# Keys, queries and values kept as hi and lo parts in DRAM between the projections and the attentions

## The chip, the cores and the metric

The kernel runs on one core of a Trainium2 chip. The metric is device time in microseconds (us) of one execution. Before the change three runs took 2356.87, 2360.24 and 2360.92 us; the median is 2360.24 us.

## The reference, cut to what matters

One layer of a streaming encoder in float32, over 1024 prompt frames and 64 sample frames; the sample frames have 512 cached frames behind them.

```python
h = x + 0.5 * post1(swiglu1(pre1(x)))                # 1024 -> 2816 -> 1024
u = pre_mix(h)
c_q, c_kv, k_r, q_sb, k_sb, v_sb = split(u @ w_in)   # 256, 128, 32, 512, 512, 512 columns
q = rmsnorm(c_q) @ w_uq                              # 8 heads of 64 + 32; the 32 are rotated by position
latent, krope = rmsnorm(c_kv), rope(k_r)             # the sample frames have the cache in front of theirs
o_mla = softmax(mask((q_nope.(latent @ w_uk) + q_rope.krope) * MLA_SCALE)) @ (latent @ w_uv)
z = q_sb.k_sb * SB_SCALE                             # 8 stick-breaking heads of 64
o_sb = exp(log_sigmoid(z) + tail) @ v_sb             # tail: sums of log_sigmoid(-z) from the later keys
h = h + post_mix(concat(rmsnorm(o_mla), rmsnorm(o_sb)) @ w_out)
y = final(h + 0.5 * post2(swiglu2(pre2(h))))
```

The new rows of latent, krope, k_sb and v_sb are outputs too.

## The kernel before

**Precision.** A float32 matmul is done as three matmuls in float32r, on a hi part (the value cast) and a lo part (the value less its hi part): hi·hi, hi·lo and lo·hi (`mm3`). `split` makes the two parts of a tile: ScalarE casts the hi part (L139, or L142 with a scale), VectorE subtracts (L140, or L143 with a scale). Whatever enters a matmul passes through a split; weights do so in each use, in pieces of 128x512 (`unit`, `weight`: load `wr`, split into `wh` and `wl`).

**Order of the work.** The tokens form two groups: the first 512 prompt frames and the 64 sample frames (576), then the other 512 prompt frames. The order is: first feed-forward of group 1, group 1's projections beside group 2's feed-forward, attention 0 (group 1: per head pair and kind two prompt heads over 512 keys and two sample heads over 576 keys), output product 0, group 2's projections, attention 1 (group 2: 16 heads over 1024 keys) beside group 1's second feed-forward, output product 1, and the dense rest. A feed-forward is a generator of single matmuls. While it serves as "filler", `wait(t)` takes matmuls from it until the kernel's own estimate of TensorE's clock reaches t; that happens wherever the code, by its written estimates, would have to wait: for a bank that is being evicted (`bank_m`, with the time that `evict(n)` puts down for n columns), and for the next step of an attention (`attend`). So the order on TensorE is set by these estimates. A tile scheduler then merges the streams of each engine.

**Queues.** Every DMA is issued by one queue, SP's, in the order of the program. A load whose buffer is still in use holds up all that stand behind it, filler weights too.

**Projections** (`project`, `cached`, `latent_kv`). A stage evicts its result to a tile `e` (four buffers) and stores it to DRAM, in full precision: `qm` (rotated queries of the latent heads), `qs` (queries of the stick-breaking heads), `kn`, `kr` (latent keys, rotated part), `ks`, `vm`, `vs` (keys and values). The cached rotated keys, keys and values are copied from DRAM to DRAM (`late`, L124 to L126). The cached latents go through `latent_kv`; its evictions are L518 and L529.

**Attention.** `load_head` loads the operands of a head, one head ahead of its use: `load_keys` loads keys into `kl`, twice, in rows 0 to 63 and again in the rows below (for latent heads the rotated part fills rows 64 to 127), and splits them into `kh` and `kl`; `load_values` loads values and splits them; `prompt_ops` and `sample_ops` load the queries and split them with the scale. Stick-breaking queries have hi in rows 0 to 63 and lo in rows 64 to 127 of one tile, so that one matmul of 128 rows serves two of the three products. Key and query tiles have 4 buffers in attention 0 and 2 in attention 1. On VectorE the splits stand in one queue with the softmax and the scan of the stick-breaking weights (`a`, L619 and L622), with the lo part of turned weights (`pl`, L680), and with the filler's splits.

Of the kernel before, what the change touches and what calls it, by code (L numbers as in the profile page):

```python
# [65 lines left out]
class Layer:  # L66
    def __init__(self, tc, ctx, a):
        self.tc, self.nc, self.a = tc, tc.nc, a
        nc = self.nc
        self.const = ctx.enter_context(tc.tile_pool(name="const", bufs=1))  # L70
        nc.scalar.preload_act_table_set("natural_log_exp_and_others")
        self.turn = 0
        self.free = [0.0] * 5
        self.busy = self.there = 0.0
        self.clock = 0.0
        self.filler = iter(())
        self.mixed = False
# [23 lines left out]
        self.qm = [scratch(f"qm_{g}", [HEADS, P, T]) for g, (_, T, _) in enumerate((G1, G2))]  # L101
        self.qs = [scratch(f"qs_{g}", [512, T]) for g, (_, T, _) in enumerate((G1, G2))]

        self.kn = [scratch(f"kn_{g}", [512, T]) for g, T in enumerate((576, 512, 512))]
        self.kr = [scratch(f"kr_{g}", [32, T]) for g, T in enumerate((576, 512, 512))]
        self.ks = [scratch(f"ks_{g}", [512, T]) for g, T in enumerate((576, 512, 512))]
        self.vm = [scratch(f"vm_{g}", [T, 512]) for g, T in enumerate((576, 512, 512))]
        self.vs = [scratch(f"vs_{g}", [T, 512]) for g, T in enumerate((576, 512, 512))]
# [8 lines left out]
    def late(self):  # L117
        nc, a = self.nc, self.a
        self.small = self.load("small", [P, 8])
        self.ident = self.load("ident", [P, P])  # L120
        self.blk = self.load("blk", [P, P])
        self.tri = self.load("tri", [P, P])
        self.osg = self.load("osg", [P, 8])
        nc.sync.dma_start(self.kr[2], a["c_kr"])  # L124
        nc.sync.dma_start(self.ks[2], a["c_k"])
        nc.sync.dma_start(self.vs[2], a["c_v"])  # L126
# [249 lines left out]
    def project(self, gi, g, hi, lo, pool, ev, tmp, at):  # L376
# [44 lines left out]
        nc.sync.dma_start(self.kr[gi], kro)  # L421


        def stick_proj(m):
            wh, wl = self.weight(pool, a["win"][3 + m])
            e = tmp()
# [5 lines left out]
            rows = slice((m % 4) * P, (m % 4) * P + P)  # L432
            if m < 4:
                nc.sync.dma_start(self.qs[gi][rows], e)
            else:
                nc.sync.dma_start(self.ks[gi][rows], e)
                nc.sync.dma_start(a["o_k"][rows, t0:t0 + T], e)

# [3 lines left out]
        for m in range(2):  # L442
# [3 lines left out]
            for h in range(4):  # L446
# [9 lines left out]
                nc.sync.dma_start(self.qm[gi][4 * m + h], e)  # L456
# [18 lines left out]
        for half in range(2):  # L475
            wv = [self.weight(pool, a["wv"][2 * half + i]) for i in range(2)]
            cols = slice(half * 256, half * 256 + 256)
            for i, n in nt:
# [11 lines left out]
                nc.sync.dma_start(self.vs[gi][i:i + n, cols], e[:n])  # L490
# [18 lines left out]
    def latent_kv(self, ev, tmp, wh, wl, lah, lal, T, C, si):  # L509
        nc = self.nc  # L510
        for m in range(4):
            e = tmp()[:, :T]
            ws = slice(m * P, m * P + P)
            for c0 in range(0, T, C):
# [3 lines left out]
                nc.any.tensor_copy(e[:, cs], ps[:, :C])  # L518
                self.evict(C)
            nc.sync.dma_start(self.kn[si][m * P:m * P + P], e)  # L520
        for i in range(0, T, P):
# [6 lines left out]
            e = tmp()[:, :512]  # L528
# [5 lines left out]
    def load_keys(self, pool, kind, h, parts):  # L534
# [4 lines left out]
        c = 0  # L539
        for src in parts:  # L540
            if kind == "mla":
                kn, kr = src
                n = kn.shape[1]
                nc.sync.dma_start(f(lo[0:64, c:c + n]), kn[h * HD:h * HD + HD])
                nc.sync.dma_start(f(lo[64:96, c:c + n]), kr)
                nc.sync.dma_start(f(lo[96:128, c:c + n]), kr)
            else:
                n = src.shape[1]
                nc.sync.dma_start(f(lo[0:64, c:c + n]), src[h * HD:h * HD + HD])
                nc.sync.dma_start(f(lo[64:128, c:c + n]), src[h * HD:h * HD + HD])  # L550
            c += n
        self.split(hi[:, :c], lo[:, :c])
        return hi, lo

    def load_values(self, pool, pair, parts):
# [4 lines left out]
        for src in parts:  # L560
            n = src.shape[0]
            full = n // P
            cols = slice(pair * P, pair * P + P)
            if full:
                for h in range(2):
                    hc = slice(pair * P + h * HD, pair * P + h * HD + HD)
                    nc.sync.dma_start(f(v[:, t:t + full, h, 1]),
                                      src[0:full * P, hc].rearrange("(t p) d -> p t d", p=P))
                    self.split(v[:, t:t + full, h, 0], v[:, t:t + full, h, 1])
            t += full  # L570
            if n % P:
                m = n % P
                nc.sync.dma_start(f(v[0:m, t, :, 1]), src[full * P:, cols].rearrange("k (h d) -> k h d", h=2))
                self.split(v[0:m, t, :, 0], v[0:m, t, :, 1])
                t += 1
# [231 lines left out]
    def load_head(self, pool, gi, pair, kind, what, par):  # L807
# [3 lines left out]
        if what == "sample":  # L811
            vsrc = [self.vm[2], self.vm[0][512:576]] if mla else [self.vs[2], self.vs[0][512:576]]
            v = self.load_values(pool, pair, vsrc)
            return [self.sample_ops(pool, mla, 2 * pair + p, p) for p in range(2)], v
        if par == 0:
            src = self.vm if mla else self.vs
            v = self.load_values(pool, pair, [src[0][0:512]] + ([src[1]] if gi else []))
        return self.prompt_ops(pool, mla, 2 * pair + par, gi), v

    def prompt_ops(self, pool, mla, h, gi):  # L820
        nc = self.nc
        if mla:
            parts = [(self.kn[0][:, 0:512], self.kr[0][:, 0:512])] + ([(self.kn[1], self.kr[1])] if gi else [])
        else:
            parts = [self.ks[0][:, 0:512]] + ([self.ks[1]] if gi else [])
        kh, kl = self.load_keys(pool, "mla" if mla else "sb", h, parts)
        ql = pool.tile([P, 512], F32R, name="ql", bufs=self.ahead)
        qh = pool.tile([P, 512], F32R, name="qh", bufs=self.ahead)
        if mla:
            nc.sync.dma_start(f(ql), self.qm[gi][h][:, 0:512])  # L830
            self.split(qh, ql, MLA_SCALE)
        else:
            rows = slice(h * HD, h * HD + HD)
            nc.sync.dma_start(f(ql[0:64]), self.qs[gi][rows, 0:512])
            nc.sync.dma_start(f(ql[64:128]), self.qs[gi][rows, 0:512])
            nc.scalar.activation(qh, f(ql), AF.Copy, scale=SB_SCALE)
            nc.vector.scalar_tensor_tensor(qh[64:128], f(ql[64:128]), SB_SCALE, f(qh[64:128]),
                                           op0=ALU.mult, op1=ALU.subtract)
# [49 lines left out]
    def sample_ops(self, pool, mla, h, par):  # L888

        nc = self.nc  # L890
        if mla:
            parts = [(self.kn[2], self.kr[2]), (self.kn[0][:, 512:576], self.kr[0][:, 512:576])]
        else:
            parts = [self.ks[2], self.ks[0][:, 512:576]]
        kh, kl = self.load_keys(pool, "mla" if mla else "sb", h, parts)
        ql = pool.tile([P, 512], F32R, name="ql", bufs=self.ahead)
# [4 lines left out]
        if mla:  # L901
            nc.gpsimd.memset(f(ql[:, zc]), 0.0)
            nc.sync.dma_start(f(ql[:, qc]), self.qm[0][h][:, 512:576])
            self.split(qh[:, qc], ql[:, qc], MLA_SCALE)
            return (qh[:, 0:P], kh), (ql[:, 0:P], kh), (qh[:, 0:P], kl)
        rows = slice(h * HD, h * HD + HD)
        nc.sync.dma_start(f(ql[0:64, qc]), self.qs[0][rows, 512:576])
        nc.sync.dma_start(f(ql[64:128, qc]), self.qs[0][rows, 512:576])
        nc.scalar.activation(qh[:, qc], f(ql[:, qc]), AF.Copy, scale=SB_SCALE)
        nc.vector.scalar_tensor_tensor(qh[64:128, qc], f(ql[64:128, qc]), SB_SCALE, f(qh[64:128, qc]),  # L910
                                       op0=ALU.mult, op1=ALU.subtract)
# [102 lines left out]
def body(tc, a, ctx):  # L1014
# [82 lines left out]
    def work(pool, T, n=4):  # L1097
# [11 lines left out]
    with tc.tile_pool(name="x0", bufs=1) as xp:  # L1109
# [26 lines left out]
        L.scaled(tmp, get, "pre1", r, *x1)  # L1136
        L.run(zero)
# [154 lines left out]
```

## Time and profile before

| | us |
|---|---|
| median of three runs | 2360.24 |
| profiled execution | 2364.98 |
| its span in the trace | 2363.2 |
| TensorE busy | 2276.1 (96%) |
| VectorE busy | 1427.0 (60%) |
| ScalarE busy | 1282.0 (54%) |
| GpSimd busy | 94.2 (4%) |

The DMA queue moved 268.79 MB, 114 GB/s over the span. The profiler saw one execution; its span lies within the time measured for it. A busy share is an average over the stretches named above: 0 to 480 us first feed-forward, 480 to 528 latent products of the cache, 528 to 672 projections of group 1, 676 to 1020 attention 0, 1210 to 1340 projections of group 2, 1345 to 1800 attention 1, and feed-forward work between and after these.

### The profile page before, as it was taken

The page shows a single profiled execution, that of the slowest core. Times are in us where ns is not written, and L with a number is a line of the kernel's source. Part 1 is how long each engine was busy: PE and PEld are TensorE (multiplying, and loading weights), DVE is VectorE, ACT ScalarE, POOL GpSimd, SP SyncE. Part 2 cuts the span into 40 slices and gives each one's busy share as a digit, 9 for nine tenths or more (in the row PEclk, how much of TensorE's full clock was granted, in tenths as well). Part 3 has the DMA queues.
Part 4 walks back from the last instruction along what each step waited for, and adds up shares of the span by engine and source line. Part 5 has one row for each costly group of instructions (what it writes and reads, how often), then busy time and mean ns, then how long its engine had stood idle before and what let it go on. Part 6 is the DMA issues. An engine that isn't in the chain of part 4 may idle for free.

```text
span 2363.2 us, 37608 instructions
## 1 busy us (share of the span) xinstructions
PE 2276.1 (96%) x13869; PEld 2045.5 (87%) x13869; DVE 1427.0 (60%) x2468; ACT 1282.0 (54%) x2494; POOL 94.2 (4%) x270
## 2 busy tenths in 40 slices
PE   8999999989999999999989999999999989999997
PEld 7999999979987777788778999989898888888885
DVE  5444444664248787755874377878776578444444
ACT  5443334453357777754542478787876445433333
POOL 1000000010000000000110000000000010000001
PEclk8999999999999999999999999999999999999998
DMA  6332222454454434344445532323212334333321
GB/s 204 100 99 85 77 90 73 151 170 135 150 153 126 131 108 125 94 153 124 133 134 184 173 99 75 104 79 98 85 60 87 119 95 140 127 98 95 98 85 36
DMA packets 186614, 268.79 MB, mean 114 GB/s; under 512 B 59216, under 2 KB 68048, under 8 KB 186400
## 3 DMA queue, kind: packets, MB, share of 16 engines
q1 hardware_dynamic: 186432, 266.41, 36.3%
q8 instruction: 109, 1.79, 0.3%
q14 instruction: 73, 0.60, 0.1%
HBM read 227.61 MB, written 40.88 MB: 114 GB/s over the span
## 4 chain that ended last, share of the span: by engine, by line
PE 71%; DVE 11%; ACT 9%; DMA 5%; issue 3%; POOL 1%; SPq 0%; DVEq 0%; ACTq 0%; POOLq 0%
PE f L154 48%; PE s L154 9%; PE v L154 6%; PE t L154 6%; DVE a L613 2%; PE t L158 2%; ACT wh L139 1%; DVE wl L140 1%; ACT a L607 1%; ACT a L609 1%; ACT a L608 1%; DVE a L610 1%; DVE e L263 1%; DVE pl L680 1%; DMA e<-h 1%
## 5 line engine op out<-in xcount | busy, mean ns | idle before, releaser
L154 PE MATMUL f<-xh,wh 128*128 128x288 f32 (+1 forms) x2112 | 695.5, 330 | 7.1 <-ACT xh L139 4.4
L154 PE MATMUL f<-xl,wh 128*128 128x288 f32 (+1 forms) x2112 | 695.9, 330 | 2.6 <-POOL xl L140 2.2
L154 PE MATMUL f<-xh,wl 128*128 128x288 f32 (+1 forms) x2112 | 695.3, 329 | 0.0
L139 ACT CAST wh<-wr 128x512 fp32r<-128x512 f32 x638 | 385.2, 619 | 523.4 <-PE f L154 352.4
L140 DVE TENSOR_TENSOR wl<-wr,wh 128x512 fp32r<-128x512 f32 x638 | 435.9, 698 | 250.6 <-ACT wh L139 217.8
L154 PEld LDWEIGHTS f<-xh,wh 128*128 128x128 f32 x2112 | 397.9, 188 | 37.9 <-ACT xh L139 5.4
L154 PEld LDWEIGHTS f<-xl,wh 128*128 128x128 f32 x2112 | 397.9, 188 | 34.4 <-POOL xl L140 4.0
L154 PEld LDWEIGHTS f<-xh,wl 128*128 128x128 f32 x2112 | 398.2, 189 | 28.4 <-issue 1.7
L154 PE MATMUL f<-hh,wh 128*128 128x288 f32 (+2 forms) x1072 | 351.6, 329 | 8.2 <-DVE y L319 8.0
L154 PE MATMUL f<-hh,wl 128*128 128x288 f32 (+2 forms) x1072 | 352.1, 329 | 0.0
L154 PE MATMUL f<-hl,wh 128*128 128x288 f32 (+2 forms) x1072 | 351.1, 328 | 0.1
L154 PEld LDWEIGHTS f<-hh,wh 128*128 128x128 f32 x1072 | 202.5, 189 | 24.0 <-DVE y L319 9.8
L154 PEld LDWEIGHTS f<-hl,wh 128*128 128x128 f32 x1072 | 202.7, 189 | 14.6 <-issue 1.0
L154 PEld LDWEIGHTS f<-hh,wl 128*128 128x128 f32 x1072 | 202.8, 189 | 13.8 <-issue 1.0
L319 DVE TENSOR_TENSOR y<-f,y 128x288 f32<-128x288 f32 (+2 forms) x248 | 126.9, 517 | 121.7 <-PE f L154 121.3
L364 DVE TENSOR_TENSOR act<-f,act 128x288 f32<-128x288 f32 (+1 forms) x132 | 70.1, 531 | 126.5 <-ACT act L363 126.4
L680 DVE TENSOR_TENSOR pl<-t,ph 128x384 fp32r<-128x384 f32 (+1 forms) x160 | 98.6, 631 | 28.6 <-ACT ph L679 27.4
L365 DVE TENSOR_TENSOR act<-f,act 128x288 f32<-128x288 f32 (+1 forms) x132 | 70.0, 531 | 65.0 <-PE f L154 61.0
L139 ACT CAST hh<-act 128x288 fp32r<-128x288 f32 (+1 forms) x132 | 65.1, 493 | 81.1 <-DVE act L365 80.8
L154 PE MATMUL v<-pl,v 128*128 128x256 f32 x320 | 89.8, 303 | 14.2 <-DVE pl L680 13.3
L679 ACT CAST ph<-t 128x384 fp32r<-128x384 f32 (+1 forms) x160 | 84.3, 543 | 33.3 <-PE t L158 31.3
L158 PE MATMUL t<-c_ident,a 128*128 128x128 f32 x616 | 91.3, 273 | 4.9 <-ACT a L624 4.8
(309 smaller groups left out, 3477.4 us busy)
## 6 DMA issues: line engine op xcount, KB each, us to landing
wr<-in_wg SPq DMA_DIRECT2D x176, 256.0 KB, 2.9
wr<-in_wu SPq DMA_DIRECT2D x176, 256.0 KB, 3.1
wr<-in_wd SPq DMA_DIRECT2D x176, 256.0 KB, 2.9
wr<-in_win SPq DMA_DIRECT2D x44, 256.0 KB, 3.2
kl<-ks SPq DMA_DIRECT2D x64, 128.0 KB, 2.9
wr<-in_wout SPq DMA_DIRECT2D x32, 256.0 KB, 3.0
h<-y SPq DMA_DIRECT2D x16, 288.0 KB, 2.3
p<-in_xT SPq DMA_DIRECT2D x16, 256.0 KB, 3.4
```

Source lines behind the costliest of these rows:

```text
L139: nc.scalar.copy(hi, x)
L140: eng.tensor_tensor(lo, x, f(hi), op=ALU.subtract)
L154: self.nc.tensor.matmul(out, lhsT=lhsT, rhs=rhs, start=start, stop=stop)
L158: self.nc.tensor.transpose(out, x, ident)
L263: self.nc.vector.scalar_tensor_tensor(x, src(k), self.gain(name, k), r, op0=ALU.mult, op1=ALU.mult)
L319: nc.vector.tensor_tensor(yy, ps[:, :C], yy, op=ALU.add)
L364: nc.vector.tensor_tensor(s, pg[:, :C], s, op=ALU.mult)
L365: nc.vector.tensor_tensor(s, pu[:, :C], s, op=ALU.mult)
L607: nc.scalar.activation(av, z, AF.Abs)
L613: nc.vector.tensor_tensor_scan(a[:, 0:n - 1][:, ::-1], zs[:, 1:n][:, ::-1], a[:, 0:n - 1][:, ::-1], BIG, op0=ALU.add, op1=ALU.subtract)
L679: nc.scalar.copy(ph[:, end:], tr[:, end:])
L680: nc.vector.tensor_tensor(pl[:, end:], tr[:, end:], f(ph[:, end:]), op=ALU.subtract)
```

## The change

Each of `qm`, `qs`, `kn`, `kr`, `ks`, `vm` and `vs` becomes a pair of DRAM tensors, a hi and a lo part. The projections split before they store (`keep`: a split and two stores, or a split straight out of the bank of the product), with the scale in the queries. The cached rotated keys, keys and values are loaded in tiles of 128 rows, split and stored (`past`), during group 1's first feed-forward. The attentions load both parts, and no longer split. The tiles `e` of the projections have eight buffers. The number of matmuls stays the same, 13,688; ScalarE's instructions go from 2428 to 2329, VectorE's from 2470 to 2380, and the DMAs of the queue from 1247 to 1644.

```diff
+    def past(self, tmp):
+        for dst, src in ((self.kr[2], a["c_kr"]), (self.ks[2], a["c_k"]), (self.vs[2], a["c_v"])):
+            for i in range(0, src.shape[0], P):
+                n = min(P, src.shape[0] - i)
+                x = tmp()[:n, :512]
+                self.nc.sync.dma_start(x, src[i:i + n])
+                self.keep([d[i:i + n] for d in dst], x, tmp)
+                yield True
+
+    def keep(self, dst, x, tmp, scale=None):
+        n, T = x.shape
+        hi, lo = (tmp()[:n, :T].bitcast(F32R) for _ in range(2))
+        self.split(hi, lo, scale, x=x)
+        self.nc.sync.dma_start(dst[0], f(hi))
+        self.nc.sync.dma_start(dst[1], f(lo))
...
         def stick_proj(m):
...
-                nc.any.tensor_copy(e[:, cs], ps[:, :C])
-                self.evict(C)
+                if m < 4:
+                    self.split(e[:, cs].bitcast(F32R), l[:, cs].bitcast(F32R), SB_SCALE, x=ps[:, :C])
+                    self.evict(2 * C)
+                else:
+                    nc.any.tensor_copy(e[:, cs], ps[:, :C])
+                    self.evict(C)
...
                     nc.vector.tensor_tensor(e[:, cs], ps[:, :C], tab[:, cs], op=ALU.mult)
                     self.evict(C)
-                nc.sync.dma_start(self.qm[gi][4 * m + h], e)
+                self.keep([d[4 * m + h] for d in self.qm[gi]], e, tmp, MLA_SCALE)
...
     def latent_kv(self, ev, tmp, wh, wl, lah, lal, T, C, si):
...
-                nc.any.tensor_copy(e[:, cs], ps[:, :C])
-                self.evict(C)
-            nc.sync.dma_start(self.kn[si][m * P:m * P + P], e)
+                self.split(e[:, cs], l[:, cs], x=ps[:, :C])
+                self.evict(2 * C)
+            for d, x in zip(self.kn[si], (e, l)):
+                nc.sync.dma_start(d[m * P:m * P + P], f(x))
...
-            nc.any.tensor_copy(e[:n], ps[:n])
-            self.evict(512)
-            nc.sync.dma_start(self.vm[si][i:i + n], e[:n])
+            self.keep([d[i:i + n] for d in self.vm[si]], ps[:n], tmp)
+            self.evict(1024)
...
-        self.split(hi[:, :c], lo[:, :c])
+        for i, t in enumerate((hi, lo)):
+            c = 0
+            for keys, rot, cols in parts:
+                n = cols.stop - cols.start
+                rows = keys[i][h * HD:h * HD + HD, cols]
+                nc.sync.dma_start(f(t[0:64, c:c + n]), rows)
+                if rot is None:
+                    nc.sync.dma_start(f(t[64:128, c:c + n]), rows)
+                else:
+                    nc.sync.dma_start(f(t[64:96, c:c + n]), rot[i][:, cols])
+                    nc.sync.dma_start(f(t[96:128, c:c + n]), rot[i][:, cols])
+                c += n
...
-    def work(pool, T, n=4):
+    def work(pool, T, n=8):
...
         L.scaled(tmp, get, "pre1", r, *x1)
+        L.run(L.past(tmp))
         L.run(zero)
```

The queue at the first pair of sample heads of attention 0, before (`vm_91`, `kn_82`, `kr_85` are the cached part, `vm_89`, `kn_80`, `kr_83` the sample frames', `in_wu` a weight of the filler):

```order
L567 DMA v<-vm_91 128x4x64 x2
L573 DMA v<-vm_89 64x2x64
L544 DMA kl<-kn_82 64x512
L545 DMA kl<-kr_85 32x512
L546 DMA kl<-kr_85 32x512
L544 DMA kl<-kn_80 64x64
L545 DMA kl<-kr_83 32x64
L546 DMA kl<-kr_83 32x64
L903 DMA ql<-qm_76 128x64
...
L296 DMA wr<-in_wu 128x512 x2
```

The same place after the change (names that end in h and l are the two parts):

```order
L594 DMA v<-vm_2h 128x4x64 x2
L594 DMA v<-vm_2l 128x4x64 x2
L597 DMA v<-vm_0h 64x2x64
L597 DMA v<-vm_0l 64x2x64
L571 DMA kh<-kn_2h 64x512
L575 DMA kh<-kr_2h 32x512
L576 DMA kh<-kr_2h 32x512
...
L571 DMA kl<-kn_2l 64x512
...
L920 DMA qh<-qm_0h 128x64
L920 DMA ql<-qm_0l 128x64
...
L316 DMA wr<-in_wu 128x512
```

Between two filler weights stand 34 issues where there were 17.

The queue in group 1's first feed-forward, where the cached tensors come in, before:

```order
L124 DMA kr_85<-in_c_kr 16x1024
L125 DMA ks_88<-in_c_k 16x16384
L126 DMA vs_94<-in_c_v 16x16384
L296 DMA wr<-in_wg 128x512 x2
L296 DMA wr<-in_wu 128x512 x2
```

After the change, somewhat later in the same feed-forward (`p` is a tile of its input stage):

```order
L316 DMA wr<-in_wg 128x512 x2
L136 DMA p<-in_c_kr 32x512
L316 DMA wr<-in_wu 128x512 x2
L145 DMA kr_2h<-p 32x512
L146 DMA kr_2l<-p 32x512
L136 DMA p<-in_c_k 128x512
L316 DMA wr<-in_wg 128x512
L145 DMA ks_2h<-p 128x512
L146 DMA ks_2l<-p 128x512
L136 DMA p<-in_c_k 128x512
```

Loads and stores of 128 rows now alternate with the weights of the filler.

ScalarE at the latent products of the cache, before (`s` and `t` are banks, `wh<-wr` a weight's cast):

```order
L139 CAST hh<-act 128x512
L518 COPY e<-s 128x512 x2
L518 COPY e<-t 128x512
L529 COPY e<-t 128x512
L529 COPY e<-s 128x512
L139 CAST wh<-wr 128x512 x2
```

After the change:

```order
L159 CAST hh<-act 128x512
L159 CAST e<-s 128x512 x2
L159 CAST e<-v 128x512
L159 CAST e<-t 128x512
L159 CAST wh<-wr 128x512
L159 CAST e<-t 128x512
L159 CAST e<-s 128x512
L159 CAST wh<-wr 128x512
```

The copies have become the casts of splits in the same order; the subtractions stand on VectorE.

## Rows read from the trace of the kernel before

**Rows 1.** The page's first part: busy us, share, instructions of each engine.

```profile
PE 2276.1 (96%) x13869; PEld 2045.5 (87%) x13869; DVE 1427.0 (60%) x2468; ACT 1282.0 (54%) x2494; POOL 94.2 (4%) x270
```

**Rows 2.** Busy time of each engine by stretch; columns in the first line.

```profile
core 0: us, PE busy (x) PEld busy (x) DVE busy (x) ACT busy (x) POOL busy (x), PEclk, DMA share, GB/s
120.00:180.00 60.00, 60.00 (x455) 60.00 (x455) 28.50 (x52) 26.66 (x55) 1.93 (x2) 1.00 0.30 93
480.00:528.00 48.00, 40.96 (x174) 32.56 (x173) 33.07 (x46) 29.18 (x52) 7.31 (x4) 0.93 0.46 154
528.00:672.00 144.00, 143.84 (x1016) 137.12 (x1015) 45.86 (x79) 46.68 (x93) 0.00 (x0) 1.00 0.44 147
676.00:1020.00 344.00, 335.88 (x1758) 270.47 (x1757) 266.29 (x556) 257.76 (x599) 17.34 (x120) 1.00 0.41 119
1210.00:1340.00 130.00, 127.26 (x706) 109.84 (x705) 52.46 (x84) 43.82 (x82) 2.96 (x2) 1.00 0.49 159
1345.00:1800.00 455.00, 436.51 (x3148) 416.01 (x3147) 354.21 (x582) 357.02 (x640) 14.22 (x93) 1.00 0.29 87
```

**Rows 3.** Waits of TensorE, 676 to 1020: us in total, times, longest.

```profile
PE s L154 <- DVE a L619: 4.5, 11, 0.7
...
PE s L154 <- DVE ql L143: 0.2, 1, 0.2
```

**Rows 4.** Waits of TensorE, 1345 to 1800.

```profile
PE v L154 <- DVE pl L680: 13.0, 24, 1.5
PE t L158 <- ACT a L624: 4.6, 4, 1.6
```

**Rows 5.** Timeline of TensorE near 766: start, length, in brackets idle before.

```profile
766.06 0.39 PE L154 MATMUL f<-hh,wh 128*128 128x512 f32 x1
766.65 0.36 PE L154 MATMUL s<-kh,qh 128*128 128x256 f32 x1 [0.20 <-DVE a L622]
```

**Rows 6.** VectorE by line and shape, 676 to 1020 (busy, mean ns, idle before).

```profile
L140 DVE TENSOR_TENSOR wl<-wr,wh 128x512 fp32r<-128x512 f32 x76 | 51.2, 680 | 5.3 <-ACT wh L139 4.8
...
L140 DVE TENSOR_TENSOR v<-v 128x256 fp32r<-128x256 f32 x32 | 12.8, 416 | 3.3 <-ACT v L139 1.7 <-DMA kl<-kr 1.4
...
L140 DVE TENSOR_TENSOR kl<-kl,kh 128x512 fp32r<-128x512 f32 x16 | 10.9, 679 | 1.7 <-ACT kh L139 1.7
```

**Rows 7.** VectorE by line and shape, 1345 to 1800.

```profile
L140 DVE TENSOR_TENSOR kl<-kl,kh 128x1024 fp32r<-128x1024 f32 x16 | 19.5, 1221 | 7.6 <-ACT kh L139 4.1 <-DMA wr<-in_wg 1.9 <-DMA kl<-kn 1.3
...
L140 DVE TENSOR_TENSOR v<-v 128x256 fp32r<-128x256 f32 x29 | 11.1, 412 | 0.6 <-ACT v L139 0.5
...
L143 DVE SCALAR_TENSOR_TENSOR ql<-ql,qh 128x512 fp32r<-128x512 f32 x8 | 5.5, 684 | 0.5 <-ACT qh L142 0.5
```

**Rows 8.** VectorE in the projections: 528 to 672, last row 1210 to 1340.

```profile
L454 DVE TENSOR_TENSOR e<-t,tab 128x288 f32<-128x288 f32 x6 | 2.7, 456 | 0.8 <-PE t L154 0.7
L140 DVE TENSOR_TENSOR ll<-e,lh 128x576 fp32r<-128x576 f32 x3 | 2.2, 759 | 0.7 <-ACT lh L139 0.7
...
L454 DVE TENSOR_TENSOR e<-t,tab 128x512 f32<-128x512 f32 x4 | 2.8, 690 | 1.2 <-PE t L154 1.2
```

**Rows 9.** Timeline of TensorE and ScalarE near 490.

```profile
491.81 0.80 PE L154 MATMUL s<-lh,wh 128*128 128x512 f32 x1 [3.81 <-ACT e L518]
...
486.87 0.62 ACT L139 CAST wh<-wr 128x512 fp32r<-128x512 f32 x1 [5.48 <-DMA wr<-in_wg]
```

**Rows 10.** SP's issues, 681 to 692; last row: KB and us to landing.

```profile
681.87 0.99 SPq L567 DMA_DIRECT2D v<-vm  x2
...
691.24 0.84 SPq L296 DMA_DIRECT2D wr<-in_wu  x2
...
kl<-ks SPq DMA_DIRECT2D x64, 128.0 KB, 2.9
```

**Rows 11.** Waits of the DMA queue, 676 to 1020.

```profile
SPq L296 <- DVE wl L140: 80.8, 32, 10.4
```

More of the change, by code (lines that the diff above doesn't have):

```diff
@@ L100, in __init__, with both @@
         self.o_s = [scratch(f"o_{g}", [D, T]) for g, (_, T, _) in enumerate((G1, G2))]
[L101 to L108, printed above, removed]
+        def both(name, shape):
+            return [scratch(name + n, shape) for n in "hl"]
+        self.qm = [both(f"qm_{g}", [HEADS, P, T]) for g, (_, T, _) in enumerate((G1, G2))]
+        self.qs = [both(f"qs_{g}", [512, T]) for g, (_, T, _) in enumerate((G1, G2))]
+        self.kn = [both(f"kn_{g}", [512, T]) for g, T in enumerate((576, 512, 512))]
+        self.kr = [both(f"kr_{g}", [32, T]) for g, T in enumerate((576, 512, 512))]
+        self.ks = [both(f"ks_{g}", [512, T]) for g, T in enumerate((576, 512, 512))]
+        self.vm = [both(f"vm_{g}", [T, 512]) for g, T in enumerate((576, 512, 512))]
+        self.vs = [both(f"vs_{g}", [T, 512]) for g, T in enumerate((576, 512, 512))]
     def load_gains(self):
@@ L420, in project @@
         nc.sync.dma_start(a["o_kr"][:, t0:t0 + T], kro)
-        nc.sync.dma_start(self.kr[gi], kro)
+        self.keep(self.kr[gi], kro, tmp)
         def stick_proj(m):
             wh, wl = self.weight(pool, a["win"][3 + m])
-            e = tmp()
+            rows = slice((m % 4) * P, (m % 4) * P + P)
+            e, l = tmp(), tmp()
             for c0 in range(0, T, C):
@@ L489, in project @@
                 self.evict(256)
-                nc.sync.dma_start(self.vs[gi][i:i + n, cols], e[:n])
+                self.keep([d[i:i + n, cols] for d in self.vs[gi]], e[:n], tmp)
                 nc.sync.dma_start(a["o_v"][t0 + i:t0 + i + n, cols], e[:n])
@@ L511, in latent_kv @@
         for m in range(4):
-            e = tmp()[:, :T]
+            e, l = (tmp()[:, :T].bitcast(F32R) for _ in range(2))
             ws = slice(m * P, m * P + P)
@@ L527, in latent_kv, with load_keys @@
             mm(ps[:n], lhsT=lah[:, i:i + n], rhs=wl[:, 512:], start=False, stop=True)
-            e = tmp()[:, :512]
-            nc.any.tensor_copy(e[:n], ps[:n])
-            self.evict(512)
-            nc.sync.dma_start(self.vm[si][i:i + n], e[:n])
-    def load_keys(self, pool, kind, h, parts):
+            self.keep([d[i:i + n] for d in self.vm[si]], ps[:n], tmp)
+            self.evict(1024)
+    def load_keys(self, pool, h, parts):
         nc = self.nc
@@ L538, in load_keys @@
         hi = pool.tile([P, self.keys], F32R, name="kh", bufs=self.ahead)
[L539 to L551, printed above, removed]
-        self.split(hi[:, :c], lo[:, :c])
+        for i, t in enumerate((hi, lo)):
[10 more added lines that the diff above has]
+                c += n
         return hi, lo
@@ L559, in load_values @@
         t = 0
-        for src in parts:
-            n = src.shape[0]
+        for vals, rows in parts:
+            n = rows.stop - rows.start
             full = n // P
             cols = slice(pair * P, pair * P + P)
[L564 to L575, printed above, removed]
+            for i, src in enumerate(vals):
+                src = src[rows]
+                if full:
+                    for h in range(2):
+                        hc = slice(pair * P + h * HD, pair * P + h * HD + HD)
+                        nc.sync.dma_start(f(v[:, t:t + full, h, i]),
+                                          src[0:full * P, hc].rearrange("(t p) d -> p t d", p=P))
+                if n % P:
+                    nc.sync.dma_start(f(v[0:n % P, t + full, :, i]),
+                                      src[full * P:, cols].rearrange("k (h d) -> k h d", h=2))
+            t += -(-n // P)
         return v
@@ L816, in load_head @@
             src = self.vm if mla else self.vs
-            v = self.load_values(pool, pair, [src[0][0:512]] + ([src[1]] if gi else []))
+            v = self.load_values(pool, pair, [(src[i], slice(0, 512)) for i in range(gi + 1)])
         return self.prompt_ops(pool, mla, 2 * pair + par, gi), v
@@ L821, in prompt_ops @@
         nc = self.nc
[L822 to L827, printed above, removed]
+        keys = self.kn if mla else self.ks
+        kh, kl = self.load_keys(pool, h, [(keys[i], self.kr[i] if mla else None, slice(0, 512)) for i in range(gi + 1)])
+        ql = pool.tile([P, 512], F32R, name="ql", bufs=self.ahead) if mla else None
         qh = pool.tile([P, 512], F32R, name="qh", bufs=self.ahead)
         if mla:
-            nc.sync.dma_start(f(ql), self.qm[gi][h][:, 0:512])
-            self.split(qh, ql, MLA_SCALE)
+            for t, d in zip((qh, ql), self.qm[gi]):
+                nc.sync.dma_start(f(t), d[h][:, 0:512])
         else:
             rows = slice(h * HD, h * HD + HD)
[L834 to L838, printed above, removed]
+            for i, d in enumerate(self.qs[gi]):
+                nc.sync.dma_start(f(qh[64 * i:64 * i + 64]), d[rows, 0:512])
         return kh, kl, qh, ql
@@ L890, in sample_ops @@
         nc = self.nc
[L891 to L896, printed above, removed]
+        keys = self.kn if mla else self.ks
+        kh, kl = self.load_keys(pool, h, [(keys[i], self.kr[i] if mla else None, c)
+                                          for i, c in ((2, slice(0, 512)), (0, slice(512, 576)))])
         qh = pool.tile([P, 512], F32R, name="qh", bufs=self.ahead)
@@ L901, in sample_ops @@
         if mla:
+            ql = pool.tile([P, 512], F32R, name="ql", bufs=self.ahead)
             nc.gpsimd.memset(f(ql[:, zc]), 0.0)
-            nc.sync.dma_start(f(ql[:, qc]), self.qm[0][h][:, 512:576])
-            self.split(qh[:, qc], ql[:, qc], MLA_SCALE)
+            for t, d in zip((qh, ql), self.qm[0]):
+                nc.sync.dma_start(f(t[:, qc]), d[h][:, 512:576])
             return (qh[:, 0:P], kh), (ql[:, 0:P], kh), (qh[:, 0:P], kl)
         rows = slice(h * HD, h * HD + HD)
[L907 to L911, printed above, removed]
+        for i, d in enumerate(self.qs[0]):
+            nc.sync.dma_start(f(qh[64 * i:64 * i + 64, qc]), d[rows, 512:576])
         return (qh[:, 0:P], kh), (qh[:, 0:P], kl)
```

17 lines of the change are left out of this document (9 added, 8 removed).

## The prediction

> **What bounds the kernel now.** I read first the busy times of the whole span: TensorE is busy 2276.1 of 2363.2 us, VectorE 60%, ScalarE 54% [rows 1]. The matmuls stay the same in number and shape, so the change can only add or remove time in which TensorE waits, some 87 us in all. Second, the engines by stretch [rows 2], to see where these waits lie: none in the dense feed-forward (60.00 of 60.00 us), 0.16 us in the first group's projections (528 to 672), 7.0 us in the step before them (480 to 528), 2.7 us in the second group's projections (1210 to 1340), 8.1 us in the first attention (676 to 1020) and 18.5 us in the second (1345 to 1800). In both attentions VectorE is busy 77 to 78% and ScalarE 75 to 78%; in the projections under 41%. Third, whom TensorE waits for in the attentions: almost always a VectorE result, the scan before the next scores (4.5 us in 11 waits) or the lo part of turned weights (13.0 us in 24) [rows 3, 4]. Fourth, single matmuls: one of 512 columns starts 0.22 to 0.23 us after the last, but across a wait that is shown as 0.20 us the next starts 0.59 us later [rows 5]: the page shows 0.16 us too little per wait. With 20 waits in the first attention and 28 in the second, the real losses are about 8.1 + 3.2 = 11.3 us and 18.5 + 4.5 = 23.0 us.
>
> **What the change removes.** In the first attention the eight VectorE rows of splits end with it: 32 of values at 416 ns, 16 of 576-wide and 16 of 512-wide keys, the prompt and sample queries; 52.3 us together, two of them in [rows 6]. VectorE falls from 266.3 to 214.0 us of 344, 77% to 62%. ScalarE loses a cast for each. In the second attention 19.5 us of keys, 11.1 us of values and two rows of 5.5 us of queries, alike, end [rows 7]: 354.2 to 312.6 us of 455, 78% to 69%. These splits are hardly waited for by themselves (TensorE waits once for one, 0.2 us, [rows 3]), so what they cost is that they stand ahead of a scan or a turned tile on VectorE's queue. I bound this from both sides: nothing, if the order of the work makes the waits; all 11.3 and 23.0 us, if load makes them. Between I take the straight line from the nearest quiet stretch, the first projections: 0.11% of idle TensorE at 32% of VectorE [rows 2], against 2.36% at 77% and 4.06% at 78%. At 62% it gives 1.6%, a third less in the first attention, 3.6 of 11.3 us; at 69% 3.3%, a fifth less in the second, 4.5 of 23.0 us. Gain: 8.1 us.
>
> **What it adds in the projections.** The splits return once per tensor, most of them in stretches where both engines have over half their time free. Most cost nothing: the key split of a 128x576 tile (0.76 us, [rows 8]) stands beside 48 matmuls of 288 columns, 6.3 us of TensorE at 0.132 us each (60 us by 455, [rows 2]). Three places are tight.
> - The query stage of the second group: 8 heads, each 6 matmuls of 512 columns, 8 x 6 x 0.225 = 10.8 us of TensorE. VectorE does 8 x 0.69 us of rotation [rows 8], now 8 x 0.69 us of scaled lo parts as well [rows 7], and four weight halves at 0.7 us [rows 6]: 13.8 us, 3.0 us over. Later projections, which ScalarE evicts, can run meanwhile: I take 2 us (0 to 3). In the first group the same sum gives 12.7 us of TensorE against 8 x (2 x 0.46 + 0.76) + 2.8 = 16.2 us, but some 5 us of filler matmuls now stand between (order): 0.5 us (0 to 3.5).
> - The latent products of the cache at 490 us. TensorE stands 3.81 us there, since ScalarE waited 5.48 us for a late weight and the evictions are behind that cast [rows 9]; neither goes. An eviction is now a cast and a subtraction, so a bank comes free 0.7 us later, once: +0.7 us.
> - The cached keys and values, before three copies from DRAM to DRAM, now 9 loads, 9 splits and 18 stores in the first feed-forward. 27 issues of the queue at 0.55 us are 15 us, spread over 16 weight loads, each good for 24 matmuls of 0.132 us, 51 us in all. TensorE has no idle time there [rows 2] and the weights run ahead: 0 (0 to 5).
>
> **What it does to the loads.** DMA issues on the SP queue from the first to the last key load of the first attention go from 276 to 448 (order). A burst of 17 takes from 681.87 to 691.24 us, 0.55 us each [rows 10]: 152 us become 246 us, of 344. The queue is in order, so a filler weight waits behind every key load ahead of it, and the burst for one sample pair doubles from 17 issues, 9.4 us, to 34, 18.7 us. Against it: today the queue stands 80.8 us in this attention only because the weight tiles are still full [rows 11], which is about the 94.6 us added, and the filler needs a unit of 12 matmuls (2.7 us) every 4.5 us (76 in 344 us, [rows 6]), with 8 split and 4 raw units of lead. A key arrives no later than before either, since the split after landing goes (cast and subtraction, 0.62 and 0.68 us, [rows 6, 9]). At the opening, where the lead is smallest, I take 1 us (0 to 9). In the second attention the issues go from 208 to 320 in some 390 us: 45%, no term.
> The Trainium skill (DMA: Bandwidth & Descriptors, "Issuing engines are not separate DMA queues") says that the time to start a DMA on the sequencer is usually small beside the DMA itself. By that rule the opening costs 0 and the sum would be 1 us better; the rows disagree: at 0.55 us per issue, six in a row outlast the landing of one key load, 2.9 us [rows 10].
>
> **Sum.** -3.6 - 4.5 + 2.0 + 0.5 + 0.7 + 1.0 = -3.9 us. The profiled execution took 2364.98 us (span 2363.2), 4.7 us above the median 2360.24 of the three runs. So 2361.1 in a profile, and 2356.3 as a median: 2356 us. A difference under 0.2%, 4.7 us, can't be told from none here.
>
> **Rivals.**
> 1. The stalls fall by more than their share (20%). If half of both losses goes, that is 17 us, and with the costs of 4.2 us, 13 us less: 2347 us. For it: the waits are on VectorE results [rows 3, 4], and splits are a fifth of VectorE's work in the first attention. Against it: in the second they fill 41.6 of 455 us, so few of its 28 waits can have met one.
> 2. The SP queue becomes the bound of the first attention (26%). Place: the change from one kind of head to the next, eight times, where values wait for a buffer and the keys and filler weights are queued behind that wait. It decides once the queue is late by more than its lead of a few units, and a queue that is busy 246 of 344 us catches up slowly. If each change costs 2.5 us of TensorE, that is 20 us, less 8.1 gained, plus 3.2: 15 us more, 2375 us; half of that is 2365 us. For it: the doubled bursts. Against it: the wait of 80.8 us, which is lead that is not used today [rows 11].
> 3. The tensors are split elsewhere but nothing moves (12%): the attentions' waits are set by the order that is written for them, which keeps its estimates of durations, and the projections hide their share. 0 to 2 us either way: 2360 us.
> 4. The forecast (42%): 2349 to 2361 us, half of it below the line of 0.2%.
>
> **Chances and range.** Faster by over 0.2%: 20% of rival 1 and 20 of the forecast's 42, 40%. Within 0.2%: 22 of the forecast and 12 of rival 3, 34%. Slower: rival 2, 26%. The range that leaves out a tenth at either end cuts the far half of rival 1 and the far third of rival 2: 2343 to 2369 us. The forecast's own range is 2349 to 2361.
>
> **What the changed profile would show.** VectorE near 62% and 69% in the attentions, ScalarE about 14 and 9 points lower than today; waits of TensorE on VectorE fewer, about 7.7 and 18.5 us lost in place of 11.3 and 23.0. In the query stages TensorE waits for the rotation's product or its bank, 2 us in the second group. The first feed-forward still without idle time. If rival 2 holds, ScalarE's casts of filler weights wait for their DMA in the first attention, and the queue no longer waits for weight tiles; TensorE then shows waits on a cast or on a key load that no VectorE row explains. The prediction is wrong if TensorE's idle time in the attentions stays as it is while VectorE's load falls as computed, or if the projections lose more than 6 us.

## The result: 60 us slower, nearly all of it in the first attention

The changed kernel took 2418.87 us (median of four runs, 2415.22 to 2421.27), the kernel before 2358.55 us beside it: a ratio of 1.0248, with a 95% interval of 1.0235 to 1.0262 (so for every ratio below). The forecast was 2356 us, its range 2343 to 2369. Of the rivals, the second named the right place and the right sign (the SP queue in the first attention), with 15 us in place of 60.

The page's first part of the changed kernel, to be read against [rows 1]:

```profile
PE 2294.3 (95%) x13869; PEld 2061.3 (85%) x13869; DVE 1390.4 (57%) x2378; ACT 1248.2 (52%) x2395; POOL 93.2 (4%) x270
```

VectorE and ScalarE have less to do, as intended, and the kernel is slower. By stretch, each cut from its first matmul to that of the next (columns as in [rows 2]): the cached latents, projections 0, attention 0, projections 1, attention 1.

```profile
482.00:513.00 31.00, 27.77 (x108) 22.01 (x108) 22.50 (x35) 21.73 (x42) 0.00 (x0) 0.89 0.68 238
513.00:691.00 178.00, 174.51 (x1151) 160.33 (x1151) 85.31 (x141) 75.65 (x149) 7.30 (x10) 1.00 0.57 187
691.00:1052.00 361.00, 316.45 (x1575) 255.04 (x1573) 206.22 (x422) 202.63 (x458) 16.95 (x117) 0.93 0.50 141
1254.00:1417.00 163.00, 158.08 (x911) 138.69 (x910) 80.87 (x128) 72.40 (x142) 6.42 (x4) 0.99 0.60 198
1417.00:1849.00 432.00, 411.33 (x2967) 393.94 (x2966) 308.83 (x507) 315.29 (x555) 14.15 (x92) 1.00 0.40 118
```

The two attentions of the kernel before, cut in the same way:

```profile
684.00:1004.00 320.00, 312.27 (x1640) 251.65 (x1639) 254.31 (x535) 242.22 (x569) 17.15 (x117) 1.00 0.41 118
1351.00:1794.00 443.00, 425.06 (x3063) 404.81 (x3062) 344.09 (x567) 347.59 (x624) 14.22 (x93) 1.00 0.29 86
```

Attention 0 takes 361 us in place of 320, with 65 matmuls fewer (filler that now runs elsewhere, some 15 us at 0.23 us each). TensorE is idle 44.6 us in place of 7.7, and its granted clock is 0.93 in place of 1.00. VectorE's load fell to 57% and TensorE waits for it all the same, for the scan 23.0 us where it was 4.5 in [rows 3] (us, times, longest):

```profile
PE s L174 <- DVE a L643: 23.0, 11, 3.1
PE v L174 <- DVE pl L704: 6.3, 5, 1.5
PE f L174 <- ACT wh L159: 3.8, 4, 1.6
```

Attention 1 is idle 20.7 us as against 17.9, with VectorE at 71%, down from 78%.

**Where an idle stretch comes from.** TensorE in the changed kernel, after the first pair of latent heads (start, length; in brackets the idle time before):

```profile
726.57 0.28 PE L174 MATMUL s<-kl,qh 128*128 128x256 f32 x1
729.51 0.58 PE L174 MATMUL s<-kh,qh 128*128 128x256 f32 x1 [2.66 <-DVE a L643]
729.89 0.41 PE L174 MATMUL s<-kl,qh 128*128 128x256 f32 x1
733.37 0.66 PE L174 MATMUL s<-kh,qh 128*128 128x384 f32 x1 [3.07 <-DVE a L643]
...
737.78 0.63 PE L174 MATMUL f<-xl,wh 128*128 128x512 f32 x1
738.20 0.63 PE L174 MATMUL f<-xh,wl 128*128 128x512 f32 x1
...
740.41 0.39 PE L174 MATMUL f<-xh,wh 128*128 128x512 f32 x1
740.64 0.39 PE L174 MATMUL f<-xl,wh 128*128 128x512 f32 x1
```

Three blocks of scores follow each other with no filler between, so TensorE stands through the whole chain from scores to scan (L643 is the scan, L619 before), 2.7 and 3.1 us. After it, matmuls of 512 columns start 0.42 us apart, at a granted clock of 0.50 (the level of 1.2 GHz), and 0.23 us apart from 739.5 on, at 1.00. In the kernel before, two score blocks at this place:

```profile
721.46 0.28 PE L154 MATMUL s<-kl,qh 128*128 128x256 f32 x1
...
726.81 0.34 PE L154 MATMUL s<-kh,qh 128*128 128x384 f32 x1
```

Seventeen matmuls of the filler stand between them, and TensorE doesn't wait. SP in the changed kernel at the same time:

```profile
724.39 0.60 SPq L856 DMA_DIRECT2D qh<-qs_0l  x1
728.83 0.34 SPq L765 DMA_DIRECT2D o<-osq  x1
729.26 0.88 SPq L316 DMA_DIRECT2D wr<-in_wg  x2
730.23 0.86 SPq L316 DMA_DIRECT2D wr<-in_wu  x2
731.18 0.93 SPq L594 DMA_DIRECT2D v<-vs_2h  x2
```

The filler's weights are issued at 729.26, behind the key and query loads and behind a store that waits for a head's result. The order of the program has changed with it: 826 filler matmuls stood between the first and the last score of attention 0, and 763 do now. The queue's own waits in attention 0 (us, times, longest), against [rows 11]:

```profile
SPq L594 <- PE v L174: 36.5, 9, 5.8
SPq L765 <- DVE osq L763: 33.2, 10, 7.6
SPq L316 <- DVE wl L160: 17.2, 17, 3.7
```

The wait for full weight tiles (L316) was this in the kernel before, in the same piece of work (684 to 1004):

```profile
SPq L296 <- DVE wl L140: 73.2, 30, 10.4
```

This wait, which the prediction took for unused lead, has fallen from 73.2 us (80.8 in the longer stretch of [rows 11]) to 17.2. Waits for a value buffer (L594) and for a finished head (L765) have grown, those for key and query buffers have shrunk: all holds other than at weights were 86 us and are 93. What grew is the time of the issues themselves, from 135 us of 320 to 224 of 361. Issues and holds together make long stretches of the queue without a filler weight: by SP's timeline the three longest, the opening included, were 16.0, 15.6 and 12.3 us before, with 12, 27 and 15 issues in them, and are 41.0, 37.6 and 31.6 us now, with 50, 52 and 54. (At the opening that is 27 and 54 between two filler weights; the 17 and 34 given with the change are the part for the sample heads.)

The lead can be counted from the timelines: filler weights issued, less those that the filler's matmuls have used up (12 of 512 columns for each), right to some two units. Its median over attention 0 was 8.5 units before and never under 3; after the change it is 1.7, and under 2 for half of the time, from the opening on. So the queue isn't late in single places: the lead, some 10 units when full, is used up at about 702 us and doesn't rise above 6 again before the end of attention 0.

### The profile page after: what moved, and what is told of

Same layout as the page of the kernel before. It is cut to its first block, busy times and chain, and to the rows that moved or that the text cites. A ratio compares the mean times of both kernels' runs of the same rounds, so it can differ in the third digit from the quotient of the medians.

```text
span 2419.5 us, 37800 instructions
## 1 busy us (share of the span) xinstructions
PE 2294.3 (95%) x13869; PEld 2061.3 (85%) x13869; DVE 1390.4 (57%) x2378; ACT 1248.2 (52%) x2395; POOL 93.2 (4%) x270
## 2 busy tenths in 40 slices
DMA packets 252665, 321.42 MB, mean 133 GB/s; under 512 B 102432, under 2 KB 113440, under 8 KB 252480
## 4 chain that ended last, share of the span: by engine, by line
PE 72%; ACT 10%; DVE 9%; DMA 4%; issue 3%; POOL 1%; SPq 0%; DVEq 0%; ACTq 0%; POOLq 0%
PE f L174 50%; PE s L174 8%; PE v L174 6%; PE t L174 6%; DVE a L637 2%; PE t L178 2%; ACT a L631 1%; ACT wh L159 1%; ACT a L632 1%; ACT a L633 1%; DVE a L634 1%; ACT z L628 1%; DVE wl L160 1%; DVE e L283 1%; DMA e<-h 1%
## 5 line engine op out<-in xcount | busy, mean ns | idle before, releaser
L174 PE MATMUL s<-kh,qh 128*128 128x256 f32 (+3 forms) x224 | 84.0, 377 | 30.6 <-DVE a L643 23.0
L703 ACT CAST ph<-t 128x384 fp32r<-128x384 f32 (+1 forms) x160 | 84.2, 543 | 37.6 <-PE t L178 37.3
```

What stands on the lines that cost most here:

```text
L174: self.nc.tensor.matmul(out, lhsT=lhsT, rhs=rhs, start=start, stop=stop)
L703: nc.scalar.copy(ph[:, end:], tr[:, end:])
```

## The experiments

Each was timed beside the kernel before on the same chip; differences are against that.

**What is taken away, alone (e5).** Attentions without splits; matmuls, loads and projections as before.

```diff
-        self.split(hi[:, :c], lo[:, :c])
-        return hi, lo
+        return lo, lo
...
-                    self.split(v[:, t:t + full, h, 0], v[:, t:t + full, h, 1])
+                    nc.gpsimd.memset(f(v[:, t:t + full, h, 0]), 0.0)
```

> The kernel before without any split in the attentions: keys and queries enter as loaded on both sides of the three products (queries unscaled), and the hi part of values is zero (set by GpSimd), so the lo parts are left out of the arithmetic; matmuls, loads and projections as before. It measures what the change takes away, without what it adds. Theory A (the order of the work makes the waits, not the load of VectorE): 2355 to 2362 us against 2360. Theory B (load makes them, as the prediction took it): 8 us less, 2350 to 2354. Theory C (each wait is a split's): 17 us less or more, below 2345.

Measured: 2356.94 us against 2359.38, ratio 0.999 (0.9981 to 1.0000). Theory A's number came. All splits of both attentions are worth 2.4 us, 0 to 4.5. VectorE's busy time over the whole run fell from 1427.0 to 1347.2 us, 79.8 of the 93.9 that the prediction had computed, and TensorE still stood idle:

```profile
681.00:992.00 311.00, 304.64 (x1618) 249.44 (x1616) 208.69 (x428) 202.35 (x462) 25.43 (x146) 1.00 0.40 120
1341.00:1785.00 444.00, 423.47 (x3068) 408.11 (x3067) 311.09 (x507) 320.01 (x567) 20.46 (x115) 0.99 0.28 86
```

Idle 6.4 and 20.5 us, against 7.7 and 17.9 in the kernel before. In attention 0 the waits for the scan fell, from 4.5 to 1.2 us (L619 before, L617 here), and others took their place. So taking this load off VectorE doesn't take the idle time away; what makes it isn't shown by this run.

**What is added to the queue, alone (e6).** The splits stay, and the second load goes to the tile that the cast fills afterwards.

```diff
-                nc.sync.dma_start(f(lo[0:64, c:c + n]), kn[h * HD:h * HD + HD])
+                for t in (hi, lo):
+                    nc.sync.dma_start(f(t[0:64, c:c + n]), kn[h * HD:h * HD + HD])
...
```

> The kernel before, its splits kept, with every key load, value load and latent query load of the attentions issued twice (296 issues more; the second goes where the cast writes its hi part afterwards). It measures what the change adds to the queue, without what it takes away. If the doubled issues are the cause: 2400 to 2430 us, with the first attention losing 60 us or more, and scores without filler between them. If it is the splits and stores in the projections: 2358 to 2368 us.

Measured: 2420.48 against 2359.38, ratio 1.0268 (1.0255 to 1.0282): 61 us, the whole loss of the change. Attention 0, with all splits still in it, has the idle time (45.0 of 371 us) and the granted clock (0.94) of the changed kernel, and the lead's median is 1.9 units; TensorE waits 15.0 us for casts of filler weights and 7.9 us for the scan:

```profile
683.00:1054.00 371.00, 326.02 (x1613) 259.18 (x1612) 255.90 (x528) 241.60 (x564) 16.80 (x117) 0.94 0.49 142
```

**What is added to the projections, alone (e7).** Projections and cached tensors of the change, attentions of before.

```diff
+            setattr(L, n, [x[0] for x in getattr(L, n)])
         L.attend(ap, 0)
```

> The projections and the cached tensors as in the change (split, stored twice), the attentions as before: they load the hi tensor as if it were the whole and split that, so the lo part is left out of the arithmetic. It measures the splits and stores in the projections alone. By the prediction's terms (2.0 + 0.5 + 0.7): 3 us more than before, 2361 to 2366. If the doubled loads weren't the cause: above 2390.

Measured: 2359.11 against 2359.38, ratio 1.0001 (0.9991 to 1.0010). The forecast of 3 us more, 2361 to 2366, is missed by 2 us. The splits and the second stores cost nothing that can be measured (at most 2.4 us).

**The queue relieved (e3).** The changed kernel, key loads on GpSimd's queue; the bytes stay (321.42 MB in both).

```diff
-                nc.sync.dma_start(f(t[0:64, c:c + n]), rows)
+                nc.gpsimd.dma_start(f(t[0:64, c:c + n]), rows)
```

> The changed kernel with the key loads (240 in the first attention) issued from GpSimd's queue; SP keeps values, queries, weights and stores. Theories A and B: 2345 to 2365 us, since SP's queue is relieved both in the scheduler's eyes and on the chip; the waits of 3 us for the scan go. Theory C: 2410 to 2420 us.

Measured: 2368.23 against 2362.51, ratio 1.0024 (1.0013 to 1.0036). That is 3 us above the range of theories A and B and far from theory C: 54 of the 60 us are gone with the keys' issues, so the bytes don't make the loss. In attention 0 the queue waits for full weight tiles as before, the lead's median is 9.2 units, and TensorE idles 7.2 of 311 us:

```profile
SPq L316 <- DVE wl L160: 82.9, 40, 10.2
...
684.00:995.00 311.00, 303.80 (x1603) 247.32 (x1602) 207.40 (x425) 204.44 (x461) 132.41 (x352) 0.99 0.70 168
```

**Order or queue?** The tile scheduler builds the order from its own estimate of when a weight is there. Is the loss made by that order, or does the queue come late on the chip? First TensorE's order of attention 0 was held as the code writes it, in the changed kernel (e1) and in the kernel before (e2).

```diff
+        if self.pinned:
+            self.tc.keep_in_program_order(ins)
```

> The changed kernel, with TensorE's instructions of the first attention held in the order in which the code writes them (in the changed kernel the tile scheduler moved scores ahead of filler matmuls there, 763 filler matmuls left between the first and the last score where the written order has 797); DMAs and splits stay. Theory A (the order is to blame: the scheduler sees filler weights late behind the doubled loads and puts bare chains of scores in their place): 2355 to 2370 us, the first attention loses 20 to 30 us instead of 75.6. Theory B (the queue is late on the chip itself): at least 2400 us, TensorE now waits for casts of filler weights. Theory C (neither order nor issues, but bytes or the splits in the projections): 2410 to 2420 us.

> The kernel before with the same pin of TensorE's order in the first attention: what the pin does by itself. All theories: within 10 us of 2358.6; theory A holds e1 against this one.

Measured: e1 2404.17, ratio 1.0176 (1.0161 to 1.0191); e2 2383.47, ratio 1.0091 (1.0076 to 1.0106). The pin itself costs 21 us, and theory A's number is missed by 34; theory B's is met, at least 2400 us with waits for casts of filler weights (18.1 us in e1). Under one order the change costs 20.7 us. That test is blunt, since the scheduler's order was better than the written one. So TensorE's instructions were chained into a given order, by order alone, without semaphores: old DMAs with the order of e6 (e9), and the changed kernel's DMAs with the order of before (e10).

```diff
+        for i, j in zip(ORDER, ORDER[1:]):
+            self.tc.add_manual_dep(self.noted[j], self.noted[i].name, ...)
```

> The kernel before, its DMAs as they are, but TensorE's 1655 instructions of the first attention chained into the order that the scheduler gave them in e6 (loads twice). If the order alone makes the loss: 2395 to 2420 us. If the queue alone does on the chip: 2360 to 2368. If both have a part, as e1 against e2 suggests (20.7 us with one order): 2375 to 2400.

> The changed kernel, its DMAs as they are, but TensorE's instructions of the first attention chained into the order that they have in the kernel before. If the order alone makes the loss: 2360 to 2370 us. If the queue alone does on the chip: 2400 or more, with TensorE waiting for casts of filler weights. If both have a part: 2375 to 2400, and the gains over e9 and e10 add up to about 60 us.

Measured: e9 2415.74 against 2360.11, ratio 1.0243 (1.0223 to 1.0262); e10 2415.25, ratio 1.0234 (1.0217 to 1.0250). Each alone costs 55 us, and together, in the changed kernel, they cost 60: they don't add up. Each lies in the range of the theory that blames it alone; that they add up to about 60, as the second expectation had it if both have a part, is out. Idle time is 45.4 of 370 us in e9 and 45.2 of 369 in e10, as in the changed kernel (44.6 of 361). No kernel was chained into its own order, so what the chain itself costs isn't measured. TensorE's waits in attention 0 of e9, and then of e10, tell why:

```profile
PE s L158 <- DVE a L633: 21.4, 12, 3.5
PE s L158 <- ACT a L649: 8.4, 11, 1.6
PE v L158 <- DVE pl L694: 8.3, 8, 1.9
```

```profile
PE f L178 <- ACT wh L163: 29.6, 6, 10.4
PE v L178 <- DVE pl L718: 4.2, 5, 1.6
```

With the old order and the new loads (e10) TensorE waits at filler matmuls for the cast of a weight. With the new order and the old loads (e9) no weight is late (the lead's median is 9.2 units), but TensorE has nothing to put between the scores. I read this as one hole, seen at two places: with late weights TensorE stands whether the order foresees it or not. SP in e10 before the longest of these waits, which ended at 987.45 us:

```profile
952.13 0.85 SPq L330 DMA_DIRECT2D wr<-in_wu  x2
954.19 0.45 SPq L585 DMA_DIRECT2D kh<-kn_2h  x1
...
983.42 0.43 SPq L934 DMA_DIRECT2D ql<-qm_0l  x1
983.95 0.85 SPq L330 DMA_DIRECT2D wr<-in_wg  x2
```

For 31 us the queue issues no weight, but the loads of a pair of sample heads and, held by their buffers, of values. At 978 us ScalarE had cast all it had, and it stood 8.4 us until the weight behind them landed. TensorE had used up the last weight by 977 us, 24 us after its issue, and stood 10.4 us.

**Issues or holds?** One DMA for both parts (e4):

```diff
-                nc.sync.dma_start(f(t[0:64, c:c + n]), rows)
+            nc.sync.dma_start(f(t[0:64, :, c:c + n]), rows)   # rows: hi and lo beside each other
```

> The changed kernel with hi and lo beside each other in DRAM, so that one DMA loads both parts of keys, values and queries: 1306 DMAs in the program instead of 1642, the same bytes. Theories A and B: 2350 to 2370 us (at the opening the scheduler still leaves a few scores without filler between them, 5 to 10 us). Theory C: 2410 to 2420 us.

Measured: 2386.1 against 2362.51, ratio 1.0090 (1.0069 to 1.0111): 24 us are left, 16 to 36 us above what both theories gave. The longest hold of the queue is the reason at one place (value loads, from 700 to 1021 us):

```profile
SPq L597 <- PE v L182: 62.2, 13, 20.2
```

From 709 to 729 us the queue stood in one value load whose buffer was still read, with filler weights behind it, and TensorE had little filler there. From 700 to 735 us TensorE idles 8.1 us at a granted clock of 0.71; from 735 to 1021 us, 11.5 of 286 us at 0.99, 4.0% as against 2.4% in the kernel before, so the rest of attention 0 ran nearly as before. The stores of finished heads, where the changed queue also stands, were moved to GpSimd's queue (e12):

```diff
-        nc.sync.dma_start(self.o_s[gi][row * P:row * P + P, c0:c0 + n], sq[:, :n])
+        nc.gpsimd.dma_start(self.o_s[gi][row * P:row * P + P, c0:c0 + n], sq[:, :n])
```

> The changed kernel with the 24 stores of finished heads (osq) on GpSimd's queue; all loads stay on SP. In the changed kernel SP stands 44 us in the first attention at these stores, waiting for VectorE's last step on a head, with filler weights behind; their own issues are 16 there, some 5.5 us. If only the time of the issues counts: 2405 to 2418 us. If such holds count as much as issues: 2375 to 2400 us.

Measured: 2406.45 against 2360.18, ratio 1.0200 (1.0183 to 1.0217). Of the 60 us some 14 go (6 to 17 by the intervals of the two ratios) with 16 of 448 issues: more than their 5.5 us and less than the 44 us of holds, though the time lies in the range given for issues alone, at its lower end. Part of the freed time went into longer holds at value loads (44.2 us in place of 36.5). That holds count beside the issues is shown at one place, in e4; here it is likely, not shown.

**Smaller versions.** Values alone, with one DMA for both parts (e8), and everything in one DMA on GpSimd's queue (e11).

```diff
-                    self.split(v[:, t:t + full, h, 0], v[:, t:t + full, h, 1])
+                nc.sync.dma_start(f(v[:, t:t + full]).rearrange("p t h i d -> p t (h i d)"), ...)
```

> Only values are split once, with the two parts beside each other in DRAM so that one DMA loads both parts of two heads: value loads fall from 72 to 40 in both attentions, 64 value splits in the attentions become 31 in the projections and 4 in the first feed-forward. If issues are what counts and splits in the attentions cost nearly nothing: 2355 to 2363 us. If the splits counted: 2350 to 2355. If splits in the projections are dear: 2362 to 2368.

Measured: 2359.84 against 2359.38, ratio 1.0008 (0.9998 to 1.0018): no difference, in the range given for the case that issues count and splits cost nearly nothing.

```diff
-            nc.sync.dma_start(f(t[0:64, :, c:c + n]), rows)
+            nc.gpsimd.dma_start(f(t[0:64, :, c:c + n]), rows)   # and all other loads of the attentions
```

> The changed kernel with both parts beside each other in DRAM (one DMA for both) and all operand loads of the attentions on GpSimd's queue; SP has only weights and stores there. Nothing is left of the doubled issues, nor can a value load that waits for its buffer hold up a weight. What e5 and e7 leave to gain is 2 us: 2354 to 2364 us. If the 20 us hold in e4 is something else than the queue: 2375 or more.

Measured: 2375.26 against 2360.11, ratio 1.0069 (1.0055 to 1.0083), a miss at the edge of what would have spoken against the queue. SP waits 131 us in attention 0 for full weight tiles, so late weights aren't the cause. TensorE's idle time is 12.0 of 307 us there and 23.8 of 430 in attention 1, as against 7.7 and 17.9 in the kernel before; why these 15 us are lost stays open. No version was faster than the kernel before, and the splits that they take out of the attentions are worth at most 4.5 us (e5).

## Why the prediction was wrong, step by step

- **The queue (+1.0 us, bounds 0 to 9): the step that failed.** Its counts held: 276 to 448 issues, and twice as many in a burst. The conclusion from [rows 11] did not. The 80.8 us were counted as if they could be spent where needed, "about the 94.6 us added". But the wait for a full tile can't be saved up: the queue can run ahead by 4 raw and 8 split units and no further. In attention 0 itself the issues take 89 us more (135 to 224) and that wait was 73.2 us: already less, before any hold. So the lead was used up in the opening and not built up again, 1.7 units in the median in place of 8.5. The 18.7 us that I had for one burst left out that bursts follow each other (27 issues at the opening became 54, 15.6 us became 31.6), and the holds between them. Measured: 61 us (e6).
- **Rival 2** had the place, the changes between kinds of heads, and the doubled burst. Its price of 2.5 us for each of eight changes was a guess; 60 us are 7.5 for each. Its remark that a queue so busy catches up slowly is what the lead shows. Two things were not in it: the lower clock after the stalls (0.93 granted in attention 0), and that the scheduler would write the lateness into the order. The difference of the orders was there to be read: 826 filler matmuls between the first and last score of attention 0 before, 763 after, and score blocks side by side. I took the order as fixed by the code's own estimates, as the section on the kernel before says; but the written order has 797 (e1, e2), so the scheduler moves matmuls, and it moves them with the loads.
- **The gain (-8.1 us)** was over-sized: 2.4 us (0 to 4.5, e5). The straight line between a quiet stretch and a loaded one had no mechanism in it. VectorE's loads in the changed kernel came out near what was computed (57% for 62%, over a longer stretch; 71% for 69%), and the waits stayed. In this rival 3 was nearer.
- **The projections (+3.2 us)**: nothing that can be measured (e7, within 2.4). The cached tensors, taken at 0, belong to this and cost nothing measurable either.
- **What was to show rival 2 wrong or right** was stated well: that the queue no longer waits for weight tiles came for the most part (73.2 to 17.2 us). The other half, waits on a cast, was 3.8 us in the changed kernel and came in size only with the old order (29.6 us, e10); I take it that the new order hides it.
- The Trainium skill's rule (DMA: Bandwidth & Descriptors, "Issuing engines are not separate DMA queues"), that starting a DMA is usually small beside the DMA, would have made the forecast worse, by 1 us: here a load lands in about 3 us, and 17 issues take 9.4 us [rows 10].

## What to carry to other kernels

Add up, for the stretch in question, what a queue issues and what it waits for: where that leaves next to no time, a prefetch that has used up its lead doesn't get it back. Time that a queue spends waiting for full buffers is no reserve beyond these buffers. Count the DMAs that stand ahead of a prefetched tile in its queue, with what they wait for. Where a scheduler orders the program by estimates, compare the orders before and after at the place in question: here the late weights showed up as waits for a scan. And taking work off a busy engine gained next to nothing here, though TensorE's waits named that engine.

## What was not expected of the hardware

The key loads on GpSimd's queue (e3) took as long to issue as on SP's, about 0.5 us each. Those of 64 and 128 KB landed in 3.5 to 5.2 us (medians) in place of 2.1 to 4.0 in the changed kernel. SP's own value loads of 128 KB landed later there too, in 3.0 to 6.5 us in place of 2.4 to 4.1, with the DMA engines busy 70% of attention 0 at 168 GB/s as against 50% at 141; so it isn't shown that the queue made the difference.

TensorE's granted clock fell to its lower level at the end of one stall of 2.66 us (changed kernel; the last three columns are the granted clock, the DMA share and GB/s):

```profile
720.00:726.00 6.00, 5.68 (x36) 4.37 (x34) 1.83 (x5) 1.26 (x4) 0.00 (x0) 1.00 0.70 207
726.00:729.50 3.50, 0.85 (x4) 0.38 (x2) 2.29 (x6) 2.53 (x7) 0.10 (x1) 0.96 0.10 32
729.50:733.40 3.90, 0.82 (x3) 0.56 (x3) 1.41 (x3) 1.74 (x5) 0.10 (x1) 0.50 0.87 279
736.00:739.00 3.00, 3.00 (x8) 2.38 (x8) 2.76 (x5) 2.43 (x7) 0.10 (x1) 0.50 0.36 79
739.50:742.00 2.50, 2.50 (x13) 2.06 (x11) 0.44 (x2) 0.36 (x1) 0.00 (x0) 1.00 0.18 41
```

TensorE was busy 95% of the 6 us before it. The next stall, of 3.07 us, lay already in the slow stretch, and TensorE was busy throughout from 733.4 us until the clock was back at 739.5.
